# New order tables for the engines of a hybrid trunk layer

## The chip, the cores and the metric

The kernel runs on one core of a Trainium2 chip. The core has TensorE (PE, with its weight loads shown as PEld), VectorE (DVE), ScalarE (ACT), GpSimd (POOL) and SyncE (SP), each with its own stream of instructions, and 16 DMA engines; here SP and POOL issue nearly all transfers. The metric is the time of one execution on the device, in microseconds.

## The reference

One layer over S = 1024 tokens of width D = 1024. A projection of the normed input feeds four groups of four heads, 64 wide: FoX attention, stick-breaking attention, RWKV-7 and RG-LRU. Each group's output is gated, an out projection brings the 1024 columns back, the input is added, and a second RMSNorm closes it. Cut to what is computed:

```
h = rms_norm(x, norm_g)
fq, fk, fv, fg, ff, sq, sk, sv, sg, rw, rg, lx, lg = split_columns(h @ w_in)
# FoX: causal softmax with cum = cumsum(log_sigmoid(ff + b))
y_fox = softmax(fq @ fk.T * scale + cum[t] - cum[s]) @ fv
# stick-breaking, s < t:  beta = sigmoid(sq @ sk.T * scale)
y_sb  = (beta[t, s] * prod over s < j < t of (1 - beta[t, j])) @ sv
# RWKV-7, per head a 64x64 state, step by step over the tokens
state = state * w_t + (state @ -kk_t) x (kk_t * a_t) + v_t x k_t;  y_t = state @ r_t
# RG-LRU: a causal convolution of width 4, gates r and i from 64-wide products
h_t = a_t * h_(t-1) + sqrt(1 - a_t^2) * (i_t * xc_t)
y = concatenate(y_fox * silu(fg), y_sb * silu(sg), y_rw * silu(rg), y_lru * silu(lg))
out = rms_norm(x + y @ w_out, final_g)
```

It is fp32 throughout. In the kernel a large product is made of three: each operand is split into a rounded part and a remainder ("h" and "l"), and h with h, h with l and l with h are summed.

## The kernel before

The kernel is written for one core in one piece. `load_w` brings a weight block (L380, DMA by POOL), rounds it on ACT (`wh`, L381) and takes the remainder on DVE (`wl`, L382). `proj` (L402, L989) multiplies: three products for each of eight pieces of D, 512 (or 256) columns wide, into a PSUM bank; the results named `pj_*` are scaled on DVE or ACT (L454, L468, `raw_*`, `sp_*`) and stored to scratch in DRAM.

RWKV-7 is computed in two halves of the tokens. For each half, products of its eight chunks of 64 tokens are prepared (`pn` L518 from N, `pg` L565, and so on), and then eight steps follow one another (`rwkv_chain`): `px` from the state UV on PE (L758), X on ACT (L767), `pu` on PE (L758), UV copied and added on DVE (L783, L796), `ph` on PE (L758), and so on. These products are 64 wide and fp32. Between them stand projection products, which fill PE while ACT and DVE work on the step.

Attention goes by blocks of 128 queries in pairs. FoX: scores `z` on PE (L1174), a reduction with the forget term on DVE (`atfox`, `mx`, L1213), `nb` from mx (L1218, L1219), exponentials on ACT (L1222), sums' reciprocal `sm` (L1226), normalisation on ACT (L1229), transposes `pt` on PE (L1246), their rounded part `PH` on ACT (L1251) and remainder `PL` on DVE (L1252), products with the values `av` (L1256), and the gated output `yp`, `yy` (L1260, L1261, L1145, L1149, L1150), which is stored to DRAM as `yx_d`.

The out projection has two parts. The first goes over the six 128-wide pieces of y that do not hold FoX, and fills PE while FoX is computed; for tokens of block tt and column half n, `yc` is its left side (L1403, two transfers by POOL, the rounded half and the remainder half, for two blocks at once), `xt` the residual tile (L1409, by POOL), `po` the sum in PSUM (L1351), and `ac = po + xt` on DVE (L1353). The FoX pieces are added at the end (`pofx`), and the closing norm squares (L1359), makes a scale `rs` (L1361 to L1374) and multiplies (L1381 on POOL, L1383 on DVE, L1385 on ACT), after which the rows are stored (L1386).

Every instruction is recorded in the order in which the program is written. At the end `in_order()` chains the instructions of each engine in the order of a table: `ORDERS` (from L56) holds for PE, DVE, Activation, Pool and SP a list of numbers, each an instruction's place among those recorded for that engine. So an engine does not choose: a transfer, an addition or a product that comes early in the table and is late in fact holds back all that stands behind it on its engine. Semaphores between the engines and buffer counts (two of `xt`, one `yc` in each of two pools) do the rest.

## Time and profile before

| | |
|---|---|
| median of 3 runs | 627.14 us (626.68 to 628.49) |
| the profiled execution, its time | 629.03 us |
| its span, mean granted clock | 627.1 us, 0.992 |
| PE busy | 608.5 us, 97% |
| DVE, ACT, POOL busy | 489.8, 390.7, 200.8 us |
| DMA | 114.35 MB, mean 182 GB/s |

The span is what the profiler saw between the first and the last instruction; the execution's time has some 2 us around it. In the lines shown further down, an instruction's row has its start, its length, the engine, the line of the code, the operation and the tiles (written from read, numbers of buffers left out), and in square brackets how long the engine had stood before it and what released it. A row of waits has the total, the count and the longest. A row of windows has the length, then the busy time and count of PE, PEld, DVE, ACT and POOL, the clock granted to TensorE (1.00 is full), the busy share of the DMA engines and GB/s.

### The profile page before, as it was taken

To read this page: it belongs to the slowest core of one execution; us is meant where nothing else is said; L and a number is where in the kernel's file an instruction comes from. 1 tells how busy PE (TensorE), PEld (TensorE's weight loads), DVE (VectorE), ACT (ScalarE), POOL (GpSimd) and SP (SyncE) were. 2 spreads that over 40 slices of the span, in tenths; PEclk is the share of its full clock that TensorE was granted. 3 is DMA by queue.
4 is the path that set the end of the run, shared out by engine and by line. 5 is a ranking of instruction groups with operands and counts; after the bars stand their busy time and mean duration, and the time that the engine had idled before them with its cause. 6 is when DMAs were issued, how large, how long until landed. Compare 5 with 4: busy or idle time off the path is not lost.

```text
span 627.1 us, 11831 instructions
## 1 busy us (share of the span) xinstructions
PE 608.5 (97%) x4060; PEld 494.9 (79%) x4060; DVE 489.8 (78%) x1131; ACT 390.7 (62%) x722; POOL 200.8 (32%) x328
## 2 busy tenths in 40 slices
PE   8999999999999999999999999999999999999993
PEld 6867777778876687777888888879997788888882
DVE  6598687998996796978866988888774776857687
ACT  6797948451013378797534776567764657766575
POOL 2231421313113675444343220400223222322175
PEclk9999999999999999999999999999999899999997
DMA  8873766527351336721998665355498867763225
GB/s 288 305 220 87 193 176 152 143 101 183 108 165 62 103 99 222 241 100 71 254 300 270 202 211 159 134 169 168 143 273 298 261 207 248 256 197 135 84 102 201
DMA packets 86403, 114.35 MB, mean 182 GB/s; under 512 B 38151, under 2 KB 57927, under 8 KB 86344
## 3 DMA queue, kind: packets, MB, share of 16 engines
q1 hardware_dynamic: 69112, 57.81, 31.0%
q0 software_dynamic: 16656, 55.23, 26.1%
q8 instruction: 32, 0.52, 0.3%
q10 hardware_dynamic: 576, 0.56, 0.3%
q14 instruction: 27, 0.22, 0.1%
HBM read 79.31 MB, written 33.21 MB: 179 GB/s over the span
## 4 chain that ended last, share of the span: by engine, by line
PE 65%; DVE 13%; ACT 7%; DMA 7%; issue 6%; POOL 2%; SPq 1%; DVEq 0%; ACTq 0%; POOLq 0%
PE po L1351 9%; PE pj_fk L402 4%; PE pofx L1351 4%; PE pj_sg L402 4%; PE pj_fq L402 3%; PE pj_sq L402 3%; PE pj_rg L402 3%; PE pj_fg L402 3%; PE zsb L1174 3%; PE avfox L1256 3%; PE pj_v L402 3%; PE zfox L1174 2%; PE avsb L1256 2%; PE ptfox L1246 2%; DMA xr<-in_xT_dram 2%
## 5 line engine op out<-in xcount | busy, mean ns | idle before, releaser
L1351 PE MATMUL po<-woh,yc 128*128 128x512 f32 x192 | 69.6, 412 | 0.0
L1190 DVE TENSOR_TENSOR_SCAN atsb<-kp,atsb 128x128 f32<-128x128 f32 (+7 forms) x32 | 43.4, 1362 | 5.1 <-ACT atsb L1188 4.9
L1351 PE MATMUL po<-wol,yc 128*128 128x512 f32 x96 | 39.8, 414 | 0.0
L1222 ACT ACTIVATE atfox<-atfox,nb 128x128 f32<-128x128 f32 (+7 forms) x32 | 24.6, 770 | 23.9 <-DVE nb L1219 12.7
L1351 PEld LDWEIGHTS po<-woh,yc 128*128 128x128 f32 x192 | 34.8, 192 | 2.9
L1187 ACT ACTIVATE kp<-zsb 128x512 f32<-128x512 f32 (+3 forms) x48 | 23.6, 491 | 17.5 <-PE zsb L1174 17.0
L1252 DVE TENSOR_TENSOR PLfox<-ptfox,PHfox 128x512 fp32r<-128x512 f32 (+1 forms) x40 | 25.4, 636 | 10.4 <-ACT PHfox L1251 9.8
L1252 DVE TENSOR_TENSOR PLsb<-ptsb,PHsb 128x512 fp32r<-128x512 f32 (+1 forms) x40 | 25.1, 630 | 8.3 <-ACT PHsb L1251 7.5
L1251 ACT ACTIVATE PHsb<-ptsb 128x512 fp32r<-128x512 f32 (+1 forms) x40 | 22.1, 555 | 10.8 <-PE avsb L1256 5.9
L1251 ACT ACTIVATE PHfox<-ptfox 128x512 fp32r<-128x512 f32 (+1 forms) x40 | 21.9, 548 | 11.1 <-PE avfox L1256 9.7
L1174 PE MATMUL zsb<-KSsb,Q 128*128 128x512 f32 (+3 forms) x96 | 28.6, 357 | 0.0
L1174 PE MATMUL zfox<-KSfox,Q 128*128 128x512 f32 (+3 forms) x96 | 25.6, 349 | 2.2 <-DVE mx L1213 2.2
L1229 ACT ACTIVATE atfox<-atfox,sm 128x128 f32<-128x128 f32 (+7 forms) x32 | 23.4, 767 | 0.7 <-DVE sm L1226 0.7
L1188 ACT ACTIVATE atsb<-zsb 128x512 f32<-128x512 f32 (+3 forms) x48 | 23.4, 488 | 0.0
L749 POOL TENSOR_TENSOR Hp<-UV,PC 64x128 f32<-64x128 f32 x32 | 16.6, 518 | 21.3 <-DVE UV L796 17.6
L1174 PEld LDWEIGHTS zfox<-KSfox,Q 128*128 128x128 f32 x96 | 17.8, 191 | 6.2 <-DVE mx L1213 2.6
L1246 PE MATMUL ptsb<-ident,atsb 128*128 128x128 f32 x144 | 22.2, 272 | 0.4 <-DVE PLsb L1252 0.4
L1381 POOL TENSOR_TENSOR ac<-ac,fg 128x512 f32<-128x512 f32 x16 | 20.7, 1324 | 5.6 <-ACT ot L1359 5.6
L1213 DVE CUSTOM_DVE_ANT_0 atfox<-zfox,Fb 128x512 f32<-128x512 f32 (+3 forms) x40 | 20.9, 524 | 2.0 <-PE zfox L1174 1.8
L1246 PEld LDWEIGHTS ptfox<-ident,atfox 128*128 128x128 f32 x144 | 18.2, 140 | 5.5
L1246 PE MATMUL ptfox<-ident,atfox 128*128 128x128 f32 x144 | 22.2, 272 | 0.0
L1256 PE MATMUL avsb<-PLsb,VS 128*128 128x256 f32 x80 | 20.1, 286 | 0.9 <-DVE PLsb L1252 0.7
(547 smaller groups left out, 2161.6 us busy)
## 6 DMA issues: line engine op xcount, KB each, us to landing
yc<-yx_d POOLq DMA_DIRECT2D x16, 768.0 KB, 6.9
xn<-in_x_dram SPq DMA_DIRECT2D x8, 512.0 KB, 5.3
Q<-p_sq SPq DMA_DIRECT2D x64, 64.0 KB, 3.4
Q<-p_fq SPq DMA_DIRECT2D x64, 64.0 KB, 3.6
xt<-in_x_dram POOLq DMA_DIRECT2D x16, 256.0 KB, 6.1
out_dram<-ac SPq DMA_DIRECT2D x15, 256.0 KB, 2.1
xr<-in_xT_dram SPq DMA_DIRECT2D x6, 512.0 KB, 9.0
wor<-in_w_out_dram SPq DMA_DIRECT2D x9, 256.0 KB, 3.8
```

The costliest lines, as they stand in the source:

```text
L402: mm = nc.tensor.matmul(out[0:ww.shape[-1]], ww, xx[hf][:, k], start=(k == 0 and xx is xh and ww is wh), stop=(k == KT - 1 and ww is wl))
L1174: ((hi - c) / 2400, nc.tensor.matmul(z[:, c - lo:hi - lo], q, k, start=j == 0, stop=j == len(ops) - 1))
L1187: nc.scalar.activation(kp[:, lo:hi], z[:, 0:hi - lo], AF.Sigmoid, scale=-0.125)
L1188: nc.scalar.activation(at[:, lo:hi], z[:, 0:hi - lo], AF.Sigmoid, scale=0.125)
L1190: nc.vector.tensor_tensor_scan(rv, kp[:, 0:n][:, ::-1], rv, 0.0, op0=ALU.mult, op1=ALU.add)
L1222: exp = nc.scalar.activation(At[qb][:, 0:n], At[qb][:, 0:n], AF.Exp, bias=nb[:, qb:qb + 1], scale=0.125, accum_out=sm_[:, 0, qb:qb + 1])
L1229: nc.scalar.activation(At[qb][:, 0:n], At[qb][:, 0:n], AF.Copy, scale=sm_[:, 1, qb:qb + 1])
L1246: T.append((P / 1200, nc.tensor.transpose(pt[:, col:col + P], At[qb][:, (2 * m + j) * P:(2 * m + j + 1) * P], ident)))
L1251: nc.scalar.activation(PH[:, 0:w], pt[:, 0:w], AF.Copy)
L1252: nc.vector.tensor_tensor(PL[:, 0:w], pt[:, 0:w], PH[:, 0:w], op=ALU.subtract)
L1256: V.append(((c1 - c0) / 2400, nc.tensor.matmul(av[:, q0:256], VS[:, 2 * m + j, :], pp[:, c0:c1], start=m == 0 and j == 0 and pi == 0, stop ...
L1351: mm = nc.tensor.matmul(po, y, w, start=i == 0, stop=i == len(ops) - 1)
```

## The change

Only `ORDERS` changes: the tables of PE, DVE, Activation and Pool are other permutations of the same instructions. The table of SP stays. PE's table takes one line more in the file, so that from there on a line number is higher by one in the kernel after. No instruction is added or taken away. The numbers themselves tell a reader nothing; a line of them:

```
-ORDERS = {...}
+ORDERS = {...}    # PE, DVE, Activation, Pool made anew; SP as it was
```

PE's order differs in the first part of the kernel, up to about 335 us of the profile, and is the same from the first attention scores on. The other engines differ in many places there, mostly by a few rows, and in some places later.

POOL where the out projection begins. `xt_5538` is the residual tile of block 0, first column half (xt00), `yc_5582` the second pair's left side (yc10, its two halves), `xt_5560` the next residual tile (xt10). Before:

```order
L1197 AFFINE_SELECT FM_6115<-Fb_5960 128x256
L1403 DMA yc_5582<-yx_d 128x6x256 x2
L1409 DMA xt_5538<-in_x_dram 128x512
L1006 DMA p_fv<-sp_fv_2980 128x512
L1409 DMA xt_5560<-in_x_dram 128x512
L1197 AFFINE_SELECT FM_6180<-Fb_5950 128x256
```

And now:

```order
L1197 AFFINE_SELECT FM_6115<-Fb_5960 128x256
L1409 DMA xt_5538<-in_x_dram 128x512
L1403 DMA yc_5582<-yx_d 128x6x256
L1006 DMA p_fv<-sp_fv_2980 128x512
L1403 DMA yc_5582<-yx_d 128x6x256
L1409 DMA xt_5560<-in_x_dram 128x512
L1197 AFFINE_SELECT FM_6180<-Fb_5950 128x256
```

The residual tile went from behind both halves of yc10 to ahead of them, and the second half of yc10 behind a store.

The residual tile went from behind both halves of yc10 to ahead of them, and the second half of yc10 behind a store.

DVE at the same place; `ac_5527` is the sum of block 0 (ac0), `nb_6134` and `sm_6121` belong to one block's softmax, `atfox_6187` to the next block's scores, `ypfox_5963` to an output of FoX. Before:

```order
L1213 ISA atfox_6128,mx_6119<-zfox_6129,FM_6115 128x128
L1213 ISA mx_6119 128x1
L1353 TENSOR_TENSOR ac_5527<-po_5540,xt_5538 128x512
L1218 TENSOR_REDUCE nb_6134<-mx_6119 128x2
L1219 TENSOR_SCALAR nb_6134<-nb_6134 128x2
L1201 MEMSET mx_6263 128x6
L1226 RECIPROCAL sm_6121<-sm_6121 128x2
L1213 ISA atfox_6187,mx_6184<-zfox_6188,Fb_5950 128x512
L1213 ISA mx_6184 128x1
L1261 TENSOR_TENSOR ypfox_5963<-avfox_6031,ypfox_5963 64x256
L1145 TENSOR_TENSOR ypfox_5963<-ypfox_5963,gt 128x256
```

And now:

```order
L1213 ISA atfox_6128,mx_6119<-zfox_6129,FM_6115 128x128
L1213 ISA mx_6119 128x1
L1218 TENSOR_REDUCE nb_6134<-mx_6119 128x2
L1219 TENSOR_SCALAR nb_6134<-nb_6134 128x2
L1201 MEMSET mx_6263 128x6
L1226 RECIPROCAL sm_6121<-sm_6121 128x2
L1261 TENSOR_TENSOR ypfox_5963<-avfox_6031,ypfox_5963 64x256
L1213 ISA atfox_6187,mx_6184<-zfox_6188,Fb_5950 128x512
L1213 ISA mx_6184 128x1
L1145 TENSOR_TENSOR ypfox_5963<-ypfox_5963,gt 128x256
L1353 TENSOR_TENSOR ac_5527<-po_5540,xt_5538 128x512
```

The addition of xt00 went from ahead of nb to eight rows further down, and one addition of ypfox went ahead of the next block's reduction.

DVE some 410 us earlier, where the tokens' second half is projected; `sp_s_903` frees the accumulator that PE's next group of products takes, and L505 is a scan of the first recurrence's preparation. Before:

```order
L490 SCALAR_TENSOR_TENSOR V_721<-raw_v_638,omu,V_721 128x512
L382 TENSOR_TENSOR wl_v0b_989<-wr_v0b_987,wh_v0b_988 128x512
L505 SCALAR_TENSOR_TENSOR SW_681<-seg,SW_681 128x520
L468 TENSOR_TENSOR sp_s_903<-pj_s_1_878,rst_bc 68x512
L468 TENSOR_TENSOR sp_k_944<-pj_k_1_919,rst_bc 128x512
```

And now:

```order
L490 SCALAR_TENSOR_TENSOR V_721<-raw_v_638,omu,V_721 128x512
L468 TENSOR_TENSOR sp_s_903<-pj_s_1_878,rst_bc 68x512
L382 TENSOR_TENSOR wl_v0b_989<-wr_v0b_987,wh_v0b_988 128x512
L468 TENSOR_TENSOR sp_k_944<-pj_k_1_919,rst_bc 128x512
L505 SCALAR_TENSOR_TENSOR SW_681<-seg,SW_681 128x520
```

Both evacuations went ahead of the scan.

In the second recurrence PE's order has other numbers of projection products between the 64-wide ones. Counted from both tables, from px of its first step on (the products between px and pu, then between pu and ph, for the eight steps in turn): before 9, 0, 16, 8, 4, 5, 4, 5 and 6, 5, 9, 7, 12, 6, 10 and none for the last, which has no ph; now 11, 8, 8, 14, 11, 9, 9, 3 and 5, 16, 7, 8, 5, 4, 4. At the end of the kernel, two output scalings on DVE (L1383) stand behind, no longer ahead of, the steps (L1371 to L1374) that make the last scale.

## The prediction

> **What bounds the kernel now.** I read the page's busy shares and its row of the clock first, then what TensorE (PE) waits for over the whole span, then the largest of those waits moment by moment, with the granted clock in windows of 2 us.

> ```profile
> PE 608.5 (97%) x4060; PEld 494.9 (79%) x4060; DVE 489.8 (78%) x1131; ACT 390.7 (62%) x722; POOL 200.8 (32%) x328
> PEclk9999999999999999999999999999999899999997
> ```

> PE is busy for 97% of 627.1 us, and the clock that it is granted is full in 38 of 40 slices: it dips in the 32nd (from 486 us on) and in the last. The change neither adds nor removes one of its products. So two things can move the time: the few us in which PE waits, and products that take longer than their own kind do elsewhere. The waits, as from, total, times, longest:

> ```profile
> PE zfox L1174 <- DVE mx L1213: 2.2, 1, 2.2
> PE pn L518 <- ACT N L516: 0.8, 1, 0.8
> PE pj_r L402 <- DVE sp_s L468: 0.4, 1, 0.4
> ```

> The largest by far is one wait of 2.2 us, where the first FoX scores after the out projection's first partial sum are formed. There:

> ```profile
> 471.66 1.70 POOL L1403 DMA_DIRECT2D yc<-yx_d  x2 [1.20 <-PE zfox L1174]
> 473.34 0.56 POOL L1409 DMA_DIRECT2D xt<-in_x_dram  x1
> 474.40 0.56 POOL L1006 DMA_DIRECT2D p_fv<-sp_fv  x1 [0.50 <-issue]
> ...
> 483.83 0.69 DVE L1353 TENSOR_TENSOR ac<-po,xt 128x512 f32<-128x512 f32 x1 [3.16 <-DMA xt<-in_x_dram]
> 484.44 0.15 DVE L1218 TENSOR_REDUCE nb<-mx 128x2 f32<-128x6 f32 x1
> ...
> 484.63 0.91 SPq L1124 DMA_DIRECT2D VS<-p_fv  x2
> ...
> 484.83 0.61 ACT L1222 ACTIVATE atfox<-atfox,nb 128x384 f32<-128x384 f32 x1 [5.43 <-DVE mx L1201]
> ...
> 486.35 0.67 DVE L1213 CUSTOM_DVE_ANT_0 atfox<-zfox,Fb 128x512 f32<-128x512 f32 x1
> ...
> 487.06 0.43 DVE L1261 TENSOR_TENSOR ypfox<-avfox,ypfox 64x256 f32<-64x256 f32 x1
> ...
> 487.09 1.22 PE L1174 MATMUL zfox<-KSfox,Q 128*128 128x512 f32 x2 [2.20 <-DVE mx L1213]
> ...
> 487.52 0.42 DVE L1145 TENSOR_TENSOR ypfox<-ypfox,gt 128x256 f32<-128x256 f32 x1
> ...
> 488.10 1.06 PE L1351 MATMUL po<-woh,yc 128*128 128x512 f32 x2
> ```

> The transfer of the residual tile (xt00) is issued behind two large yc transfers at 473.34 and ends only when `ac0 = po + xt00` can start, at 483.83. VectorE (DVE) has then stood for 3.16 us with nb, the next mx and the next score reduction queued behind that one instruction. ACT's exponentials wait for nb (5.43 us), the next reduction on DVE waits for them, and PE waits for a score bank: 2.20 us. The clock, which is the first number behind POOL's group, then falls:

> ```profile
> 484.00:486.00 2.00, 0.88 (x6) 0.45 (x4) 0.76 (x4) 1.17 (x3) 0.55 (x1) 1.00 0.28 96
> 486.00:488.00 2.00, 0.91 (x2) 0.82 (x3) 1.63 (x6) 1.95 (x6) 0.00 (x0) 0.73 0.95 300
> 488.00:490.00 2.00, 2.00 (x8) 1.72 (x8) 2.00 (x6) 1.05 (x3) 0.96 (x2) 0.50 0.76 234
> 490.00:492.00 2.00, 2.00 (x13) 1.72 (x12) 1.86 (x9) 0.17 (x1) 1.52 (x3) 0.91 0.76 217
> ```

> Granted 0.73, 0.50 and 0.91 in three windows of 2 us, PE lost 0.54 + 1.00 + 0.18 = 1.7 us more. So this one late transfer costs about 3.9 us.

> [...]

> **The change, part by part.** All durations are of the profiled execution: 629.03 us, with a span of 627.1, so 1.9 us lie around the span. The median of the three runs is 627.14, so that execution was 1.9 us long, and I put the differences on the median.

> *The out projection's start (479 to 492 us).* POOL issues xt00 ahead of both halves of yc10; on DVE, `ac0` goes behind nb, the next mx, a reciprocal, a ypfox addition, the next reduction and a ypfox product. Transfers from these two places have taken, minimum, median and maximum (yc, then xt):

> ```profile
> DMA to landing us min/median/max: 5.0/7.1/10.3
> DMA to landing us min/median/max: 3.2/7.2/10.5
> ```

> Issued at about 471.7, xt00 lands between 474.9 and 482.2, by the ends of the xt row; both are early enough, as follows. DVE is free for nb at 480.67 (483.83 - 3.16) instead of 484.44. From nb to PE's restart there were 2.65 us (484.44 to 487.09); a ypfox addition of 0.43 us now stands in that path, so the score bank is free at about 483.75. PE comes to these scores at 484.89 (487.09 - 2.20), hence without a wait. Then DVE does the ypfox product (0.42) and ac0 (0.69), done by about 484.8, and PE, which wants the accumulator at about 485.4 (484.89 and two scores at full clock), does not wait for it either. Gain: 2.2 + 1.7, and 0.2 of a smaller wait just ahead of it, since ACT now splits that ptfox before a normalisation:

> ```profile
> 480.04 0.38 PE L1256 MATMUL avfox<-PLfox,VS 128*128 128x256 f32 x1 [0.21 <-DVE PLfox L1252]
> ```

> Against it stands what was moved back: the second half of yc10. Before it was issued at about 472.5 and, at the row's maximum of 10.3, there at 482.8. Now xt00 and a p_fv store go ahead, so it is issued at about 473.9 and, with the queue as slow, there at 484.2. PE wants it some 0.3 us after 485.4. But SP's VS and Q loads, which started at 484.63, wait for that p_fv store; it lands earlier now, so they start up to 3 us earlier and share the engines with the end of the yc10 half and with xt10 behind it. Bounds of this wait: 0 (it lands at 484.2) and 2.2 (3 us of shared transfers, half of them the others', 1.5, and behind xt10, as late, an addition of 0.69 on DVE). I take 0.4, near the lower end, since the DMA share was already 0.28 in 484 to 486, so the queue does drain. The stage: -4.1 + 0.4 = -3.7.

> *A wait of 0.45 us at 68.4.* On DVE the evacuation sp_s (L468) stood behind a 1.43 us scan and is now ahead of it and of wl_v0b:

> ```profile
> 66.31 1.43 DVE L505 TENSOR_TENSOR_SCAN SW<-seg,SW 128x520 f32<-128x520 bf16 x1 [1.23 <-ACT SW L503]
> 67.67 0.66 DVE L468 TENSOR_TENSOR sp_s<-pj_s,rst_bc 68x512 f32<-68x512 f32 x1
> ...
> 68.39 0.50 PE L402 MATMUL pj_r<-xh,wh_r0b 128*128 128x512 f32 x1 [0.45 <-DVE sp_s L468]
> ```

> The scan itself waited 1.23 us for ACT, so sp_s fits into that hole. -0.45; the scan becomes at most 0.66 later, and what hangs on it, pn01's chain, has 9 more projection products ahead of it on PE. At 43.06 (pn, 0.8 us) ACT makes N a little earlier: between 0 and -0.8, I take -0.2, since the DVE product it needs hardly moves.

> *The recurrence (181 to 213 and 260 to 297 us), on PE.* A visit of the 64-wide fp32 products of L758 between projection products costs PE a switch on both sides:

> ```profile
> 269.87 0.28 PE L989 MATMUL pj_sv<-wh_sv,xh 128*128 128x256 f32 x1
> 269.99 0.28 PE L989 MATMUL pj_sv<-wh_sv,xl 128*128 128x256 f32 x1
> 270.20 0.45 PE L758 MATMUL px<-UV,GM 128*64 128x64 f32 x8
> 270.48 0.40 PE L758 MATMUL py<-UV,GM 128*64 128x64 f32 x8
> 270.81 0.39 PE L989 MATMUL pj_sv<-wl_sv,xh 128*128 128x256 f32 x1
> 271.03 0.28 PE L989 MATMUL pj_sv<-wh_sv,xh 128*128 128x256 f32 x1
> ```

> Projection products start 0.12 us apart, but the visit starts 0.21 behind the last of them, and the first one after it takes 0.22 to the next: about 0.2 us more, and some 0.1 more for the drain of the last small product, so 0.3 a visit. Counted in the order, the visits of L758 go from 47 to 48, and the runs of all such small products from 67 to 70. So runs are not longer in this count: +0.9 us; bounds +0.3 (one visit) and +0.9.

> In the second half the waits were:

> ```profile
> PE ph L758 <- DVE UV L783: 0.6, 2, 0.3
> PE pu L758 <- ACT X L767: 0.4, 1, 0.4
> PE px L758 <- DVE UV L796: 0.3, 2, 0.2
> ```

> The visit in which pu followed px directly now has 8 projection products between them, which covers the 0.4. Between px and pu the others go from 4 to 16 products to 3 to 14, and between pu and ph from 6 to 12 down to 4, 4, 5, 5 and 7 in five of the seven steps that have a ph. Each is 0.12 us (0.23 for a 512-wide one), and the work on DVE and ACT between takes about 1.3 us or, where the linear unit's scan stands on DVE, more; the order moves several of these away. Waits there: between 0 (all cover) and 2.4 (0.6 at four short places); I take 1.0, so -0.3.

> *The tail.* On DVE two output scalings (2.55 us beside POOL's product) go behind the four small steps that made the last scale:

> ```profile
> 619.48 2.55 DVE L1383 TENSOR_SCALAR ac<-ac,rs 128x512 f32<-128x512 f32 x2
> 621.95 0.14 DVE L1371 TENSOR_SCALAR rsq<-rsq 128x1 f32<-128x1 f32 x1
> ...
> 622.81 0.72 ACT L1385 ACTIVATE ac<-ac,rs 128x512 f32<-128x512 f32 x1 [1.92 <-DVE rs L1374]
> ```

> The wide work remains, and SP still issues the stores one after another: between 0 and -0.8 (622.50 back to about 621.7); I take -0.4. From 335 us to 471 PE's order is identical and the others' nearly; the first 33 us wait for transfers that did not move. Both I cost at nothing.

> Sum: -3.7 - 0.45 - 0.2 + 0.9 - 0.3 - 0.4 = -4.15, from 627.14 to 623.0.

> **Rivals.** *The stall moves to the next transfer.* What speaks for it: SP's loads starting up to 3 us earlier, the DMA share of 0.95 in 486 to 488, and DVE now reaching xt10's addition early. With 2.0 us of wait at 485.7 the stage gives back 1.6 more than I took, but the clock holds: 627.14 - 4.15 + 1.6 = 624.6; from 2.2 us on the clock can fall as before, another 1.7: 626.3. [...]

> *The order does little.* If the new places are as mis-set for the real landing times as the old ones, waits of the same total arise elsewhere: 33 to 335 us hold nearly all of the moved rows, and those small waits together were under 4 us. If 0.05 us were added at each of the 70 small-product runs, that is 3.5 us, and the time is 626.5. For it speaks that short fills between pu and ph grow shorter; against it, that most moved rows are a place or two away.

> *The clock falls all the same.* If the dip at 487 us has another cause than the wait (the transfers that come at full share from 486 on, say), its 1.7 us stay: 624.7. Against it: transfers had a share of 1.01 from 480 to 482 at a clock of 1.00, in the row below. [...]

> ```profile
> 480.00:482.00 2.00, 1.96 (x10) 1.71 (x11) 0.67 (x4) 0.00 (x0) 0.41 (x1) 1.00 1.01 406
> ```

> *Slower: the handoffs of the second recurrence.* Fifteen handoffs there (eight px to pu, seven pu to ph) depend on how many projection products lie between. If each waits 0.5 us, about as long as pj_r above waits for DVE, that is 7.5 us where I took 1.0: 629.5. It decides from 0.47 each on; at the longest of today (0.38) the time is 627.7. Against it: those from px to pu mostly have more cover than before, so nearly all of it would have to come from the seven.

> **How the numbers follow.** 0.3% is 1.9 us, about what a measurement of this kernel can tell from no change. My forecast has 0.53, with its own range 621.3 to 624.5; the stall moves 0.18, of which a third is within 0.3%; the clock falls all the same 0.05; the order does little 0.15, nearly all within 0.3%; slower handoffs 0.09, most of it long enough to be slower by over 0.3%. Faster: 0.53 + 0.12 + 0.05 + 0.03 = 0.73; slower 0.07; within 0.3% the remaining 0.20. The range reaches from the lower ends (stage -4.1, pj_r -0.45, pn -0.8, tail -0.8, recurrence -1.3, visits +0.3, so -7.15, hardly all at once: 620.8) to the stall that moves with its clock (626.3) and the order that does little (626.5), and a little beyond, 627.2; about one in ten lies on the far side of each end.

> **What would show it.** Around 480 to 490 us: xt00 landing before 482.5, `ac` (L1353) on DVE without its DMA wait, no wait of zfox on mx over 0.5 us, the clock at 1.00 in all windows. If instead po waits for yc, or `ac` for the second xt, the first rival holds. At 68 us no wait of pj_r on sp_s. Between 260 and 297 us, waits of ph on UV up, of pu on X gone. I am wrong if PE's busy time in the first 335 us grows by more than 1 us, or if PE's waits there sum to more than before.

## The result: slower, and where the profile after shows it

The median of six executions of the kernel after is 636.32 us (633.46 to 641.03), that of six of the kernel before 627.11; the ratio is 1.015, with a 95% interval of 1.0113 to 1.0188. The forecast was 623.0. The profiled execution of the kernel after took 633.46 us, with a span of 631.5. Of the 9.2 us between the medians, the two profiled executions show 4.4: the one before lies 1.9 us above its median, the one after 2.9 below. Line numbers are the same in both kernels, not higher by one in the kernel after: L1252 is the remainder PL in both.

The page after, its busy line and its row of the clock:

```profile
PE 608.0 (96%) x4060; PEld 494.2 (78%) x4060; DVE 492.5 (78%) x1131; ACT 390.4 (62%) x722; POOL 201.9 (32%) x328
PEclk9999999999999999999999899999999999999998
```

PE's own work is what it was (608.5 before). The dip of the clock has gone from the 32nd slice, and a new one stands in the 23rd, from 347 us on. What PE waited for, as total, times, longest:

```profile
PE avsb L1256 <- ACT PHsb L1251: 3.1, 1, 3.1
PE ptsb L1246 <- DVE PLsb L1252: 2.1, 1, 2.1
PE px L758 <- DVE UV L796: 1.7, 6, 0.4
PE ph L758 <- DVE UV L783: 1.5, 3, 0.7
...
PE px L758 <- POOL z_sv L981: 0.8, 1, 0.8
```

The wait of zfox on mx (2.2) is not there any more, nor those of pn and pj_r. In their place stand two long ones, in the stick-breaking attention, where the forecast had put nothing, and more waits in the recurrence. PE's waits in the first 335 us sum to 6.0 us, and to 4.3 in the kernel before; the forecast had named this as a sign of being wrong.

Read at the same PE instructions in both traces, the kernel after is ahead by 1.9 us at 103 us (103.04 before, 101.12 after), behind by 1.6 when the first scores begin (334.70, 336.33), behind by 7.3 when the projection of fk begins (349.95, 357.24), by 9.0 at the first ptfox (472.24, 481.21), and by 4.4 in the middle of the out projection (507.70, 512.09) and at the end (627.1, 631.5). So the stage that the forecast looked at gave 4.6 us; the place at 474 us, the one at 352 us and the recurrence took 1.7 + 5.7 + 3.5.

**At 352 us.** `kp` (L1187) and `atsb` (L1188) are ACT's steps on the stick-breaking scores, and `PHsb` is the rounded part that PE's product `avsb` needs. The chain of events in the kernel after, in order of time:

```profile
347.29 0.54 POOL L970 DMA_DIRECT2D p_fq<-sh_fq  x1 [7.47 <-ACT wh_fk L381]
...
350.76 0.63 ACT L969 ACTIVATE sh_fq<-sp_fq 128x512 fp32r<-128x512 f32 x1 [3.96 <-DMA p_fq<-sh_fq]
351.30 0.47 ACT L1187 ACTIVATE kp<-zsb 128x384 f32<-128x384 f32 x1
...
351.67 0.48 ACT L1251 ACTIVATE PHsb<-ptsb 128x384 fp32r<-128x384 f32 x1
...
352.30 0.35 PE L1256 MATMUL avsb<-PHsb,VS 128*128 128x256 f32 x1 [3.12 <-ACT PHsb L1251]
...
353.24 0.58 PE L1256 MATMUL avsb<-PLsb,VS 128*128 128x256 f32 x1 [0.59 <-DMA Q<-p_sq]
```

and the two ACT rows in the kernel before:

```profile
346.31 0.49 ACT L1251 ACTIVATE PHsb<-ptsb 128x384 fp32r<-128x384 f32 x1
...
350.67 0.67 ACT L969 ACTIVATE sh_fq<-sp_fq 128x512 fp32r<-128x512 f32 x1
```

sh_fq10, the rounded part of the third piece of fq, needs one of three buffers that are free only when an earlier piece has been stored. It ran at nearly the same time in both kernels (350.67, 350.76). Before, it stood behind eleven rows of ACT that now stand behind it, the first kp and PHsb among them, and these are held for 3.96 us. It is the same fault as that of xt00 on DVE, at another place: an instruction whose transfer is late, placed too early on an engine that keeps its order. The store in the first row is itself late: the `sh_fq` that it stores was done at 344.36 (343.73 + 0.63), 2.9 us before. The kernel before has the same 2.9 us (339.24 to 342.16), so the wh_fk in the brackets does not explain them, and what does is not shown. The clock follows:

```profile
350.00:352.00 2.00, 0.00 (x0) 0.00 (x0) 0.58 (x1) 1.24 (x3) 0.32 (x1) 1.00 0.84 278
352.00:354.00 2.00, 1.11 (x5) 0.95 (x5) 2.00 (x5) 1.51 (x4) 1.31 (x3) 0.77 0.73 241
354.00:356.00 2.00, 2.00 (x9) 1.83 (x9) 1.48 (x3) 1.09 (x3) 0.00 (x0) 0.50 0.94 269
356.00:358.00 2.00, 2.00 (x11) 1.69 (x10) 1.42 (x2) 1.68 (x4) 0.00 (x0) 0.88 0.40 115
```

0.46 + 1.00 + 0.24 = 1.7 us of clock, with the wait of 3.1 and 0.6 more at the next product: 5.4 of the 5.7.

**At 474 us.** POOL forms the mask FM when the load of Fb has landed, DVE's reduction needs FM, and in the new order the two PLsb that PE needs stand behind that reduction:

```profile
472.38 0.76 POOL L1197 TENSOR_SCALAR_AFFINE_SELECT FM<-Fb 128x256 f32<-128x256 f32 x2 [7.77 <-DMA Fb<-F_d]
...
472.81 0.29 DVE L1213 CUSTOM_DVE_ANT_0 atfox<-zfox,FM 128x128 f32<-128x128 f32 x1 [2.20 <-POOL FM L1197]
...
473.02 1.28 DVE L1252 TENSOR_TENSOR PLsb<-ptsb,PHsb 128x512 fp32r<-128x512 f32 x2
...
473.86 0.63 PE L1246 MATMUL ptsb<-ident,atsb 128*128 128x128 f32 x4 [2.10 <-DVE PLsb L1252]
```

The clock stayed full behind this wait, at 1.00 in each window of 2 us from 472 to 480 us. Before, the same two PLsb went first, and PE waited for nothing that stood behind the reduction:

```profile
464.06 1.29 DVE L1252 TENSOR_TENSOR PLsb<-ptsb,PHsb 128x512 fp32r<-128x512 f32 x2 [0.75 <-ACT PHsb L1251]
...
466.92 0.29 DVE L1213 CUSTOM_DVE_ANT_0 atfox<-zfox,FM 128x128 f32<-128x128 f32 x1 [1.50 <-POOL FM L1197]
```

**At the out projection's start** it went as forecast: ac0 has no wait in its row, and the clock is full.

```profile
492.69 0.68 DVE L1353 TENSOR_TENSOR ac<-po,xt 128x512 f32<-128x512 f32 x1
```

```profile
490.00:492.00 2.00, 2.00 (x13) 1.69 (x12) 0.86 (x3) 1.95 (x7) 0.00 (x0) 1.00 0.94 331
492.00:494.00 2.00, 2.00 (x12) 1.44 (x10) 2.00 (x6) 1.66 (x4) 0.33 (x1) 1.00 0.93 283
```

### The profile page after: what moved, and what is told of

Read it like the earlier page. It is cut to its first block, busy times and chain, and to the rows that moved or that the text cites. A ratio compares the mean times of both kernels' runs of the same rounds, so it can differ in the third digit from the quotient of the medians.

```text
span 631.5 us, 11823 instructions
## 1 busy us (share of the span) xinstructions
PE 608.0 (96%) x4060; PEld 494.2 (78%) x4060; DVE 492.5 (78%) x1131; ACT 390.4 (62%) x722; POOL 201.9 (32%) x328
## 4 chain that ended last, share of the span: by engine, by line
PE 71%; DVE 10%; DMA 6%; issue 5%; POOL 3%; ACT 3%; SPq 1%; DVEq 0%; POOLq 0%; ACTq 0%
PE po L1351 11%; PE pj_fk L402 4%; PE pj_k L402 4%; PE pj_r L402 4%; PE pj_rg L402 3%; PE pj_lx L402 3%; PE pj_v L402 3%; PE pj_fg L402 3%; PE zsb L1174 3%; PE avfox L1256 3%; PE pj_fv L989 3%; PE avsb L1256 3%; PE zfox L1174 3%; PE pj_lg L402 3%; PE ptfox L1246 2%
## 5 line engine op out<-in xcount | busy, mean ns | idle before, releaser
L1351 PE MATMUL po<-woh,yc 128*128 128x512 f32 x192 | 69.1, 409 | 0.0
L1351 PE MATMUL po<-wol,yc 128*128 128x512 f32 x96 | 39.5, 411 | 0.0
L1351 PEld LDWEIGHTS po<-woh,yc 128*128 128x128 f32 x192 | 34.3, 189 | 2.9
L1222 ACT ACTIVATE atfox<-atfox,nb 128x128 f32<-128x128 f32 (+7 forms) x32 | 24.6, 770 | 18.8 <-DVE nb L1219 10.4
L1252 DVE TENSOR_TENSOR PLfox<-ptfox,PHfox 128x512 fp32r<-128x512 f32 (+1 forms) x40 | 25.4, 636 | 12.0 <-ACT PHfox L1251 11.5
L1187 ACT ACTIVATE kp<-zsb 128x512 f32<-128x512 f32 (+3 forms) x48 | 23.5, 490 | 14.9 <-PE zsb L1174 14.2
L1252 DVE TENSOR_TENSOR PLsb<-ptsb,PHsb 128x512 fp32r<-128x512 f32 (+1 forms) x40 | 25.2, 631 | 9.2 <-ACT PHsb L1251 8.3
L1174 PE MATMUL zsb<-KSsb,Q 128*128 128x512 f32 (+3 forms) x96 | 29.3, 364 | 0.0
L1174 PE MATMUL zfox<-KSfox,Q 128*128 128x512 f32 (+3 forms) x96 | 25.0, 342 | 0.0
L749 POOL TENSOR_TENSOR Hp<-UV,PC 64x128 f32<-64x128 f32 x32 | 18.5, 578 | 19.9 <-DVE UV L796 18.2
L1188 ACT ACTIVATE atsb<-zsb 128x512 f32<-128x512 f32 (+3 forms) x48 | 23.4, 488 | 0.0
L1256 PE MATMUL avsb<-PHsb,VS 128*128 128x256 f32 x80 | 20.2, 273 | 3.1 <-ACT PHsb L1251 3.1
L1213 DVE CUSTOM_DVE_ANT_0 atfox<-zfox,Fb 128x512 f32<-128x512 f32 (+3 forms) x40 | 20.9, 523 | 1.7 <-PE zfox L1174 1.6
L1246 PEld LDWEIGHTS ptsb<-ident,atsb 128*128 128x128 f32 x144 | 17.8, 141 | 5.6 <-issue 2.3
```

The costliest lines, as they stand in the source:

```text
L1174: ((hi - c) / 2400, nc.tensor.matmul(z[:, c - lo:hi - lo], q, k, start=j == 0, stop=j == len(ops) - 1))
L1187: nc.scalar.activation(kp[:, lo:hi], z[:, 0:hi - lo], AF.Sigmoid, scale=-0.125)
L1188: nc.scalar.activation(at[:, lo:hi], z[:, 0:hi - lo], AF.Sigmoid, scale=0.125)
L1222: exp = nc.scalar.activation(At[qb][:, 0:n], At[qb][:, 0:n], AF.Exp, bias=nb[:, qb:qb + 1], scale=0.125, accum_out=sm_[:, 0, qb:qb + 1])
L1246: T.append((P / 1200, nc.tensor.transpose(pt[:, col:col + P], At[qb][:, (2 * m + j) * P:(2 * m + j + 1) * P], ident)))
L1252: nc.vector.tensor_tensor(PL[:, 0:w], pt[:, 0:w], PH[:, 0:w], op=ALU.subtract)
```

## The experiments

The edits are given as rows of an engine's order, with what moved marked. The kernel before had medians of 627.1 to 627.8 beside them, and a single execution of 625.96 us beside the last three.

**One late step put back.**

```
 ACT   wh_fk1_0 <- wr_fk1_0
-ACT   sh_fq10 <- sp_fq10
 ACT   kp02 <- zsb020
 ACT   PHsb000 <- ptsb000
...
 ACT   atsb13 <- zsb130
+ACT   sh_fq10 <- sp_fq10
```

(and on DVE its subtraction behind the next piece's evacuation, on POOL a weight load ahead of its stores)

> The kernel after, with one step put back as it stood before: on ACT sh_fq10 (L969) behind the weights of blocks 02 to 13 again, on DVE its remainder (L971) and on POOL its two stores accordingly. Theory (one late transfer holds ACT): PE's wait at 352 us (3.1 + 0.6 us and the half clock behind it, 5.7 us in all in the profile after) is gone, so about 5.5 us less than the kernel after: 628 to 631. Rival (the sp buffers are short whatever the order): the wait goes to the next sh_fq, at most 2 us gained: 632 or more.

Measured: 629.87 us (1.0037 of before, 1.001 to 1.0063), 6.5 less than the kernel after. PE's waits on PHsb are gone; in the profiled execution the wait at PLsb is 3.3 us. The store is as late there as in the kernel after, and sh_fq10 runs later still, but PHsb no longer stands behind it:

```profile
347.80 0.54 POOL L970 DMA_DIRECT2D p_fq<-sh_fq  x1 [6.04 <-ACT wh_fk L381]
...
349.52 0.49 ACT L1251 ACTIVATE PHsb<-ptsb 128x384 fp32r<-128x384 f32 x1
...
353.88 0.67 ACT L969 ACTIVATE sh_fq<-sp_fq 128x512 fp32r<-128x512 f32 x1
```

So it is the place of this step in the orders that cost the time, not the late store by itself.

**The other late step put back.**

```
-DVE   atfox10, mx10 <- zfox100, FM10
 DVE   PLsb330 <- ptsb330, PHsb330
 DVE   PLsb331 <- ptsb331, PHsb331
 DVE   sm_00 <- sm_00
+DVE   atfox10, mx10 <- zfox100, FM10
```

> The kernel after, with one row moved: on DVE the reduction of atfox10 with FM10 (L1213), which waits for POOL's FM and so for the load of Fb, goes behind two PLsb and a reciprocal again. Theory (one late load holds DVE): PE's wait at 474 us (2.1 us) is gone, 1.7 to 2.2 us less than the kernel after, more where the clock fell behind it in some executions. Rival (PE would wait for PHsb or the scores there anyway): under 0.5 us.

Measured: 632.68 us (1.0071, 1.0046 to 1.0096), 3.6 less than the kernel after. The profile of the kernel after had 2.1 us of wait there; other executions wait longer at this place, as shown below.

**Both put back.**

> Both of the two steps put back. If the two add up: 7.4 us less than the kernel after in the undisturbed case, 626 to 628, level with the kernel before: the gain of the out projection's start (4.6) and of the first 100 us (1.9) is then eaten by the recurrence (3.5) and the rest (under 1). Rival (the two stalls share their time, the second only exists because PE comes later or earlier there): less than the sum, 629 or more.

Measured: 626.68 us (0.9979, 0.996 to 0.9999), 9.6 less than the kernel after, where the two alone gave 6.5 and 3.6. So nearly all of the sum adds up, and these two steps are as much as the whole loss against the kernel before. The kernel after did not run beside these three. Taken against the kernel before beside each, the differences are 7.1, 4.3 and 10.3 us, and by the widths of the intervals each is uncertain by some 3 us. What PE still waits for from 335 to 500 us:

```profile
PE avsb L1256 <- DVE PLsb L1252: 0.7, 1, 0.7
PE ptsb L1246 <- DVE PLsb L1252: 0.4, 1, 0.4
```

**The recurrence alone.** The kernel before with the rows that ran from 103 to 334 us in the new order, on PE, DVE, ACT and POOL.

> The kernel before, with only the rows that ran between 103 and 334 us (all four engines) in the order of the kernel after. Theory (the new order of the recurrence is worse by itself): 3.5 us slower than before, 630.6, from waits of px and ph on UV and from three more small-product runs. Rival (it is worse only because PE reaches it 1.9 us earlier with the same transfers): within 1.0 of before.

Measured: 631.15 us (1.0059, 1.0036 to 1.0081), 3.4 slower, as the theory said. Its waits from 178 to 335 us:

```profile
PE px L758 <- DVE UV L796: 1.6, 6, 0.4
PE pj_fq L402 <- ACT wh_fq L381: 1.0, 1, 1.0
PE ph L758 <- DVE UV L783: 0.9, 2, 0.6
PE px L758 <- POOL z_sv L981: 0.8, 1, 0.8
PE lg L1056 <- DVE xs L1050: 0.3, 1, 0.3
```

These are 4.6 us, against 0.7 + 0.5 + 0.4 before. That is 3.0 us more, and with 0.9 for three more runs of small products 3.9, within the interval of what was measured (2.3 to 5.1).

**The second recurrence alone** (225 to 334 us).

> The kernel before, with only the rows that ran between 225 and 334 us in the order of the kernel after (the second recurrence). From the profile of the run with both recurrences, 2.0 to 2.5 of its 3.4 us lie here: 2.2 us slower than before. Rival (the first recurrence's waits of ph on UV carry the most): under 1.2.

Measured: 628.48 us (1.0028, 1.0005 to 1.0051), 1.4 slower. The interval holds both the 2.2 of the theory and the rival's 1.2, so how the 3.4 us divide is not settled.

**A price by itself: more visits.** On PE of the kernel before, at 13 steps (at a fourteenth the product moved is a `pg`, 64 rows by 128, one of the small ones itself):

```
 PE    ph <- UV, BKT
+PE    pj <- (a projection product)
 PE    py <- UV, GM
-PE    pj <- (the same)
 PE    px <- UV, GM
```

> The kernel before, with one row moved on PE in 13 of the steps of both recurrences: a projection product that stood behind ph and py now stands between them, so that one visit of 64-wide products becomes two; what lies between ph and the next px is the same in all. Theory (a visit costs PE 0.3 us): 3.9 us slower than before. Rival (the switch is hidden where PE waits anyway, or costs 0.2): 1.5 to 2.6 us.

Measured: 631.03 us (1.0062, 1.0035 to 1.0088), 3.9 slower: 0.30 us a visit, with 0.17 to 0.42 by the interval, which holds the rival's 0.2 as well. The trace narrows it. Projection products start 0.23 us apart, but the 64-wide ones start 0.32 behind the last of them, and from the single one between ph and py to the next start it takes 0.43:

```profile
187.18 0.40 PE L402 MATMUL pj_sq<-xh,wh_sq 128*128 128x512 f32 x1
187.41 0.39 PE L402 MATMUL pj_sq<-xl,wh_sq 128*128 128x512 f32 x1
187.73 0.45 PE L758 MATMUL ph<-UV,BKT 128*64 128x64 f32 x8
188.11 0.50 PE L402 MATMUL pj_sq<-xh,wl_sq 128*128 128x512 f32 x1
188.54 0.45 PE L758 MATMUL py<-UV,GM 128*64 128x64 f32 x8
```

From ph to py it is 0.81 us here, and 0.28 in the kernel before, where py follows ph directly. Less the 0.23 that the product between them takes anywhere, 0.30 us are left.

**The out projection's two rows, together and apart**, in the kernel before: on POOL xt00 ahead of both halves of yc10, on DVE ac0 behind the next reduction and the ypfox product.

> The kernel before, with two rows moved as the change moves them: on POOL the transfer of xt00 ahead of both halves of yc10, on DVE the addition ac0 behind the next reduction and a ypfox product. Theory (the late xt00 held DVE, and the clock fell from the wait): 4.1 us less than before, with no wait of zfox on mx and a clock of 1.00 there. Rival (the clock falls anyway, or the stall goes to yc10's second half): 2.2 us or less.

> Of these two rows the one on POOL alone; ac0 stays ahead of nb on DVE. If the landing time alone is what matters, all of the 4 us; xt00 would land by 478 to 482, DVE reaches ac0 at 480.7. If not, ac0 still waits for up to 1.5 us and some 2 us are gained.

> Of these two rows the one on DVE alone; xt00 stays behind both halves of yc10 and lands at 483.8. By the sum of the rows DVE reaches ac0 at 484.1, just behind that landing, so nearly all of the 4 us should be gained too. Rival: the engines' transfers are then late for PE at the next accumulator, and 1 to 2 us of wait stay.

Measured: both rows 625.54 us (0.9967, 0.9949 to 0.9985), POOL's alone 626.18 (0.9975, 0.9959 to 0.9992), DVE's alone 625.88 (0.9976, 0.9956 to 0.9995): 2.0, 1.3 and 1.6 less than before. None is the 4 us of the first theory, and the intervals do not separate the three. The profiled executions show where the stall went. With xt00 first, alone or not, DVE no longer waits, but PE waits for VS, a load of SP that is issued less than 1 us before xt00. It lands 9.8 us after its issue with both rows and 9.5 with POOL's alone, against 6.7 in the kernel before and 7.4 with DVE's alone; that the two transfers delay each other is the author's estimate from these four times. This is the row of the kernel with both edits:

```profile
481.44 0.35 PE L1256 MATMUL avfox<-PHfox,VS 128*128 128x256 f32 x1 [2.27 <-DMA VS<-p_fv]
```

With POOL's row alone the wait is 2.1 us, with the half clock behind it. With DVE's row alone, the transfer stays late and nobody waits for it: from 470 to 500 us only two waits of 0.2 us are left.

```profile
PE avfox L1256 <- ACT PHfox L1251: 0.2, 1, 0.2
PE avfox L1256 <- DVE PLfox L1252: 0.2, 1, 0.2
```

Between 472 and 507 us PE gained 2.2 us on the profile before with both rows, 0.8 with POOL's and 3.7 with DVE's. So by the traces the row on DVE is the one that matters, and moving the transfer moved a stall from DVE's queue to SP's; the medians do not show it. In the kernel after, POOL also puts a store between yc10's halves and PE arrives later, and this wait does not appear.

**The first 103 us alone.**

> The kernel before, with only the rows that ran in the first 103 us in the order of the kernel after. From the two profiles (PE 1.9 us ahead at 103 us): 1.9 us less than before. Rival: PE reaches the middle part earlier and waits there instead, within 0.7 of before.

Measured: 627.13 us (0.9994, 0.998 to 1.0009): nothing that can be told from none, which fits the rival and not the 1.9 us of the theory. PE was 1.8 us ahead of the profile before at 103 us here too. But in the profiled executions of five edits that leave the first 103 us alone (the last three, the second recurrence, more visits) it was ahead by 0.6 to 1.3 as well, and in a sixth (the recurrence alone) 0.2 behind. So some 0.7 us of that lead, the mean of the six, is a late start of the profiled execution before.

**Repaired versions.** The kernel after with both steps back and the recurrence as before; and the kernel before with the first 103 us of the kernel after and DVE's ac0 later.

> The kernel after, with the two steps that stall put back and with the rows of 103 to 334 us (the recurrence) as before. If the parts add up (both steps back 626.7, the recurrence 3.4): 623.3, about 4 us less than before. Rival (transfers collide elsewhere once the recurrence is faster): 625 or more.

> The kernel before, with the first 103 us as in the kernel after and ac0 later on DVE, and nothing else. From the two single runs (0.4 and 1.6 less than before): 625.5, 2 us less than before.

Measured: 626.08 us (0.9997, 0.9977 to 1.0017) and 626.25 (0.9979, 0.9963 to 0.9996). The first missed its 623.3: its profiled execution took 624.1 with no wait over 0.7 us after the start, but half of its executions had mean clocks of 0.990 to 0.993 and a median of 628.1. From the kernel with both steps put back it differs in the recurrence alone. Its ratio is no lower than that one's 0.9979, though the recurrence cost 3.4 us in the kernel before and the two profiled executions are 2.5 us apart (626.64 and 624.11); so the parts do not simply add up, and why is open. Of all versions, the one with the out projection's two rows in the kernel before has the lowest ratio, 0.9967; its interval overlaps those of the next four.

**Further executions of the kernel after and of the repaired one.**

> The kernel after once more, for the profile of another execution. The six times of it run from 633.5 to 641.0 with a mean granted clock from 0.993 down to 0.983, and the profile shows only the fastest. Theory (the two waits at 352 and 474 us are longer or bring the half clock with them in some executions): a slower execution has a second stretch of 0.50 behind 474 us, or a longer one behind 352. Rival: a third wait somewhere else, not in the profile so far.

> The kernel after a third time, as in the run before this one: theory and rival are the same (a second stretch of half clock behind 474 us or a longer one behind 352, or a third wait elsewhere).

> The repaired kernel after once more: its times run from 624.1 (clock 0.996) to 629.8 (0.990), and the profile shows the fastest. Expected in a slower execution: a stretch of half clock behind a wait that the fast one lacks; if none, the spread lies in the first 30 us, where transfers are waited for.

Measured: 634.95, 633.31 and 623.71 us. The first two show that the two places change from execution to execution: the wait at 474 us was 3.3 us in one, without a dip of the clock, and 3.2 in the other, with one. At 352 us it was the other way round: 1.0 and 0.6 us of wait with a dip in the first, 1.7 us without one in the second. The place at 352 us took 3.1 and 2.2 us by PE's position and that at 474 us 2.8 and 4.4, where the first profile had 5.7 and 1.7. These are the windows of the second at 474 us:

```profile
472.00:474.00 2.00, 2.00 (x15) 2.00 (x14) 0.48 (x3) 1.73 (x4) 0.50 (x1) 0.69 1.00 314
474.00:476.00 2.00, 2.00 (x12) 2.00 (x11) 0.35 (x1) 0.14 (x1) 0.00 (x0) 0.50 0.86 274
476.00:478.00 2.00, 2.00 (x18) 2.00 (x18) 1.53 (x8) 0.49 (x1) 0.41 (x1) 0.95 0.23 71
```

No third place with a dip was found. Executions of 638 us and more were not profiled, so that they have the dip at both places is likely from their clock of 0.983 to 0.986, but not shown. The third, of the repaired kernel, has no dip before the end; what its longer executions lose stays unexplained.

## Why the prediction was wrong, step by step

- **"From 335 us to 471 PE's order is identical and the others' nearly ... Both I cost at nothing."** This step failed. Nearly is not enough: sh_fq10 moved by eleven places on ACT and one reduction by three on DVE. Instead of nothing they cost 6.5 and 3.6 us, 9.6 together, by the medians, and 5.7 and 1.7 us in the first profile after. The forecast read xt00 as a late transfer ahead of others on an engine in order, and did not ask the same of every other instruction that waits for a transfer in the new tables. With 3.4 us more for the recurrence, and less 0.4 for the first 103 us and 1.3 to 2.0 for the out projection's rows, the parts add up to 10.6 to 11.3 us, for 9.2 measured.
- **The stage at 479 to 492 us, -3.7.** The mechanism was right: the wait and the dip are gone, and the stage is 4.6 us shorter in the two traces. Its size against the median was wrong: 1.3 to 2.0 in the kernel before. With the stage's order unchanged, the wait of zfox on mx was 1.6 and 1.8 us with a full clock in two profiled executions (the first 103 us alone, the recurrence alone), and 1.8 and 2.8 us with the half clock in two others (the second recurrence, more visits). So the 1.7 us of clock belonged to some executions and not to all. With them and some 0.7 us of a late start, the profiled execution lay 1.9 us above the median, and the differences were put on the median all the same. Of 95 executions of the kernel before beside the experiments, 24 had a mean clock of 0.993 or less, like the profiled one; the others had 0.994 to 0.996, and medians 1.2 to 2.2 us lower.
- **The rival that the stall moves** was set aside at 0.4 us; in the kernel before with the two rows, it was 2.3 us, at VS on PE, not at yc10.
- **pj_r, -0.45, and pn, -0.2:** both waits are gone in the kernel after. That of pn is gone as well in the profiled executions of the out projection's edits, which leave its order alone, so it belonged to that execution. The first 103 us together were worth 0.4 us of the median, within the noise.
- **Visits, +0.9:** the price of 0.3 us is confirmed by the trace (0.30).
- **The second recurrence's waits, -0.3:** wrong in sign. The wait of pu on X went, as said, and those of ph on UV fell (0.6 to 0.3) where they were to rise. But px waits for UV's addition (L796) five times there, 1.6 us in all where it was 0.3, the handoff from ph to the next px, which the forecast had left out when it counted px to pu and pu to ph. Beside it stands a wait for z_sv on POOL (0.8) and, in the kernels with the recurrence alone, one of pj_fq (1.0). The first recurrence, whose waits the forecast passed over, adds 1.0 us of waits of ph on UV (1.2, from 0.2). With the visits the recurrence was put at 0.6 us and measured 3.4.
- **The tail, -0.4:** from the last pofx to the end it takes 10.14 us now and took 10.40 before. But the second half of PE's pofx products ahead of it took 0.5 us longer (11.63 now, 11.15 before), so nothing is left.
- **The rivals.** "The order does little" had the right reason, that new places are as mis-set for the real landings as the old, but it looked only at 33 to 335 us and at a sum under 4 us. The slower rival had its place in the recurrence, where about a third of the loss lies, and its mechanism, waits at the handoffs, is what came.

## What to carry to other kernels

Where every engine keeps a fixed order, list first the instructions that wait for a transfer, ask for each who is behind it if the transfer comes some us later, and compare that list in the old order and the new. In the traces here, moving the waiting instruction back left no wait over 0.2 us (from 470 to 500 us), while with the transfer moved forward another landed later (VS, 9.5 to 9.8 us after its issue, from 6.7), though the medians of the two do not differ clearly. And a stall that the profiled execution shows, its clock above all, belongs to that execution: before it is credited to the median, ask how many of the runs have it.

## What the runs showed of the hardware

The half clock came with waits of PE and nowhere else in the middle of the kernel, but not with every one. In the 17 profiled executions, between 30 and 600 us, it came with a wait of 2.2 us (the kernel before), 3.1 (the kernel after, at 352 us), 3.3 (the first step put back), 2.8 (the other put back), 1.8 (the second recurrence alone), 2.8 (more visits), 2.1 (xt00 first alone), 3.2 (the kernel after a third time, at 474 us), and with 1.0 and 0.6 us one behind the other (the kernel after once more, at 352 us). It did not come with 1.6 (the first 103 us alone), 1.7 (the kernel after a third time, at 352 us), 1.8 (both recurrences alone), 2.1 (the kernel after, at 474 us), 2.3 (the out projection's two rows) nor 3.3 (the kernel after once more, at 474 us), nor with any shorter wait that stood by itself. The mean granted clock of the nine executions that have it is 0.990 to 0.993, that of the other eight 0.994 to 0.996. The windows of the last-named, and of xt00 first alone:

```profile
472.00:474.00 2.00, 0.00 (x0) 0.00 (x0) 0.16 (x1) 0.18 (x2) 0.59 (x2) 1.00 0.52 162
474.00:476.00 2.00, 1.11 (x10) 1.14 (x11) 1.41 (x5) 0.56 (x2) 1.77 (x4) 1.00 0.37 130
```

```profile
480.00:482.00 2.00, 1.38 (x7) 1.28 (x8) 0.75 (x4) 1.19 (x3) 0.96 (x2) 0.84 1.02 409
482.00:484.00 2.00, 2.00 (x7) 1.42 (x6) 0.84 (x3) 1.22 (x4) 0.00 (x0) 0.50 0.86 320
```

The switch from the wide projection products to 64-wide fp32 ones and back costs PE 0.30 us a visit in the trace with more visits. And two transfers of one size did not take the same time: of two loads of Fb (512 KB each) in the kernel after, one landed 3.6 us after its issue at 456.0, with a DMA share of 0.57 to 0.69 in the windows from 456 to 462 us, and the other, issued at 460.8, kept POOL waiting for 7.77 us, until 472.4, while the DMA share was 1.00 to 1.05 in the windows from 462 to 472 us.
